# Sums of weight blocks: two of four made by a plain and an accumulating transfer instead of on VectorE, with the lower row of blocks counted as negated

## The chip, the cores and the metric

One core of one Trainium2 chip runs one program. The metric is device time in microseconds of one execution, as the median of several runs. All arithmetic is in 32-bit floats; the matmuls take their operands as a high and a low part (type fp32r), so that each product of two matrices is three passes: high by high, low by high and high by low.

## The reference

Two groups of requests (512 and 256 tokens, 768 in all, width 1024) run through a trunk of two layers. Each layer has a feed-forward block (SwiGLU) ahead of and behind a mixer. The change touches only the four feed-forward blocks.

```python
def swiglu(h, wg, wu, wd):                  # wg, wu: 1024 x 2816; wd: 2816 x 1024
    return (jax.nn.silu(h @ wg) * (h @ wu)) @ wd

def even_layer(x, ...):                     # the odd layer is alike, with another mixer
    x = x + 0.5 * swiglu(rmsnorm(x, f1_n), f1_g, f1_u, f1_d)
    x = x + mixer_ab(rmsnorm(x, mix_n), ...)
    x = x + 0.5 * swiglu(rmsnorm(x, f2_n), f2_g, f2_u, f2_d)
    return x
```

## The kernel before

**Layout.** The activations lie transposed: 8 tiles of 128 features by 768 tokens (`x0` to `x7`), cut into two halves of 384 tokens. The feed-forward width of 2816 is worked in 11 pairs of 2 x 128 columns (function `pair`); behind every second pair a stage `down` multiplies what two pairs (the first time one) left by their rows of the down matrix. The last two pairs go through `down_last`, in the ordinary way.

**Seven products instead of eight.** Within a pair, a weight matrix is a 2 x 2 arrangement of blocks `a11`, `a12` (upper row: the first 128 output columns, by the two halves of the 1024 inputs) and `a21`, `a22` (lower row: the second 128 output columns). A block is 128 x 512 floats, 256 KB. With the activations cut in 2 x 2 as well, Winograd's form of Strassen's method needs seven block products, named p1 to p7 in the code, each with one weight operand and one activation operand (`b11`, `b21`, `t1`, `t2`, `t3`, `b22`, `n4`). Three of the weight operands are blocks (`a11`, `a12`, `a22`), four are sums of blocks, which VectorE makes in the function `sums` (line 579 of the profile):

```python
s1 = a21 + a22;   s2 = s1 - a11;   s3 = a11 - a21;   s4 = a12 - s2
```

A pair needs them for the gate and the up matrix, a `down` stage for its pairs, so a full stage makes eight sums. Each operand then is split in a high part (`whi`, ScalarE, L115) and a low part (`wlo`, VectorE, L116) ahead of its 12 matmuls per matrix.

**Buffers.** The weight blocks arrive from memory in tiles `raw` of 512 KB (four buffers; two blocks of one row of the arrangement per tile). The sums lie in tiles `s` (eight buffers, handed out in turn). The split parts lie in `whi` and `wlo` (five buffers each). All transfers are issued by SyncE (queue SP), in one order; a transfer into a buffer waits until the readers of what was in it are done, and what stands behind it in the queue waits with it.

**The beginning of a block.** The first three pairs are early: their products p1 and p2 run on the first token half while the norm is still being worked out, in the order of the table `ORDER`; then each goes through p6, p7, p5, p3, p4. The later pairs go p1, p6, p2, p7, p5, p3, p4 (the very last in an order of its own). The norm's scale comes from a matmul with ones (`ps_aux<-ones,acc`), a small VectorE step and a power on GpSimd (`sm<-sm,minus`, L254), and three transposes on TensorE (`ps_aux<-ident,sm`, L152).

**Order of the work.** TensorE's order is written out by the program (a planner with generators and delays). The other engines' orders come from a scheduler that knows which values each instruction needs and estimates when they are there.

Of the kernel before, what the change touches and what calls it, by code (L numbers as in the profile page):

```python
# [48 lines left out]
class Trunk:  # L49
# [54 lines left out]

    def wsplit(self, src, eng=None, keep=False):
# [8 lines left out]
        hi, lo = (t.rearrange("p (a b) -> p a b", a=src.shape[1]) for t in (hi, lo))  # L114
        nc.scalar.copy(hi, src)  # L115
        (eng or nc.gpsimd).tensor_tensor(out=lo, in0=src, in1=hi.bitcast(F32), op=ALU.subtract)  # L116
        return hi, lo
# [179 lines left out]
    def feed(self, m, h):  # L297


        nc = self.nc  # L300
        c0, c1 = HALVES[h]
        k = m % 4
        x = self.x[m][:, c0:c1]
        if h == 0:
            self.gain_split("b11" if m < 4 else "b21", k, x, m)
            return
        if "work" not in self.guards:
            self.unfed.append(m)
            return
        t = self.tmp[m] = self.etile("tmp")  # L310
        if m < 4:
            nc.vector.tensor_tensor(out=t, in0=x, in1=self.x[m][:, :H], op=ALU.subtract)
        else:
            nc.scalar.activation(t, x, AF.Copy, scale=self.gain(m))
        if k in self.tmp and k + 4 in self.tmp:
            t2 = self.tmp["t2", k] = self.etile("tmp")
            self.combine(t2, self.tmp[k], -1, k, self.tmp[k + 4])
            self.split(*self.b["t2"][k], t2)
            if len(self.tmp) == KD + 4:
                self.made += ["t2"]  # L320

    def gain_split(self, n, k, src, m):

        hi, lo = self.b[n][k]
        self.nc.scalar.activation(hi, src, AF.Copy, scale=self.gain(m))
        self.nc.vector.scalar_tensor_tensor(
            out=lo, in0=src, scalar=self.gain(m), in1=hi.bitcast(F32), op0=ALU.mult, op1=ALU.subtract
        )

    def combine(self, out, x, sign, m, other):  # L330

        g, op = (self.gain(m), ALU.subtract) if sign > 0 else (self.gain(m, self.ngains), ALU.add)
        self.nc.vector.scalar_tensor_tensor(out=out, in0=x, scalar=g, in1=other, op0=ALU.mult, op1=op)  # L333
# [10 lines left out]
    def rest(self, after):  # L344
# [5 lines left out]
        for n in ("t3", "t1", "b22", "n4"):  # L350
            for k in range(4):
                with self.tc.issue_after(self.copied[after - 1]) if after else nullcontext():
# [6 lines left out]
                    elif n == "n4":  # L359
                        t = self.tmp["t2", k]  # L360
                        self.combine(t, self.x[k + 4][:, a0:a1], 1, k + 4, t)
# [27 lines left out]
    def ffn(self, pre):  # L389
# [8 lines left out]
        d, dl = {}, {}  # L398

        def operands(q):  # L400


            h = hs.pop(q)
            sub = lambda o, x, y: nc.vector.tensor_tensor(out=o, in0=x, in1=y, op=ALU.subtract)
            d[q] = {}
# [6 lines left out]
            yield put("b11", h11)  # L412
            yield sub(h11, h12, h11)
            yield put("t1", h11)
            yield put("b21", h21)
            yield sub(h11, h22, h11)
            if q and q % 2 == 0:
                self.later = operands_2(h, sub, put)
                return
            for _ in operands_2(h, sub, put):  # L420
                yield

        def operands_2(h, sub, put):
            h11, h12, h21, h22 = h[0, 0], h[0, 1], h[1, 0], h[1, 1]
# [3 lines left out]
            yield put("b22", h22)  # L428
            yield sub(h21, h21, h11)
            yield put("n4", h21)  # L430

        def pair(p):
# [5 lines left out]
            def load(tiles):  # L438
                for n in names:
                    for i in tiles:  # L440
                        r = self.first.pop(0) if self.first else self.raw(f"{pre}_w_{n}", 0, KD, (2 * p + i) * P, P)
                        a[n, i + 1, 1], a[n, i + 1, 2] = r[:, 0:4, :], r[:, 4:8, :]

# [4 lines left out]
            def sums(n, name):  # L448
                return self.sums(a[n, 1, 1], a[n, 1, 2], a[n, 2, 1], a[n, 2, 2], s, n, name)

# [23 lines left out]
            def hidden(i, half, g, u):  # L474
# [5 lines left out]
                nc.vector.tensor_tensor(out=t, in0=g, in1=r, op=ALU.mult)  # L480
                nc.scalar.activation(t, t, AF.Silu)
                nc.vector.tensor_tensor(out=v, in0=u, in1=r, op=ALU.mult)
                nc.vector.scalar_tensor_tensor(out=t, in0=t, scalar=0.5, in1=v, op0=ALU.mult, op1=ALU.mult)  # L483

# [51 lines left out]
            if early:  # L536
# [6 lines left out]
                yield  # L543
            load((0, 1))
            if p:
# [30 lines left out]

    def sums(self, a11, a12, a21, a22, s, n, name):

        f = lambda o, x, y, op: self.nc.vector.tensor_tensor(out=o, in0=x, in1=y, op=op)  # L579
        if name == "s1":  # L580
            return s[n, "s1"]
        if name == "s4":
            t = s[n, "s2"]
            f(t, a12, t, ALU.subtract)
            return t
# [3 lines left out]
        t = s[n, name] = self.fw.tile([P, 4, P], F32, tag="s", name=name, bufs=8)  # L589
        if name == "s3":  # L590
            f(t, a11, a21, ALU.subtract)
        else:
            f(t, s[n, "s1"], a11, ALU.subtract)
        return t

    def dtile(self, name):
        return self.fw.tile([P, H], F32R, tag="e", name=f"d{name}", bufs=NE)

    def down(self, pre, pairs, d, acc):
# [3 lines left out]
        nc = self.nc  # L603
        a, s, bank = {}, {}, {}
        for p in pairs:
            rows = [self.raw(f"{pre}_w_down", 2 * p + k, 1, 0, D)[:, 0, :] for k in (0, 1)]
            a[p] = [t[:, i * 512 : (i + 1) * 512].rearrange("p (a b) -> p a b", a=4) for i in (0, 1) for t in rows]
        sums = lambda name: {p: self.sums(*a[p], s, p, name) for p in pairs}
# [27 lines left out]

        w = {n: {p: a[p][i] for p in pairs} for i, n in enumerate(("a11", "a12", "a21", "a22"))}
        s2 = sums("s2")
# [11 lines left out]
    def last_operands(self, d, k0, h, acc=None):  # L650

        todo = [(j, o) for o in ((0, 1), (1, 1)) for j in range(4)] if acc else []
        for half in (0, 1):
            for i in (0, 1):
# [3 lines left out]
                for j, (f, g) in todo[:3]:  # L658
                    x = self.x[4 * f + j][:, HALVES[g][0] : HALVES[g][1]]
                    self.nc.vector.tensor_tensor(out=x, in0=x, in1=acc[j], op=ALU.add)  # L660
                    yield
# [936 lines left out]
```

## Time and profile before

| | |
|---|---|
| median of 3 runs | 2640.08 us (2638.77 to 2641.93) |
| the profiled execution | 2645.25 us, its span 2643.5 us |
| granted TensorE clock, mean | 0.993 |
| TensorE busy | 2586.7 us, 98% |
| VectorE busy | 2225.4 us, 84% |
| ScalarE busy | 1357.5 us, 51% |
| GpSimd busy | 97.6 us, 4% |
| moved by transfers | 214.27 MB, mean 81 GB/s |

Busy is the time between the start and the end of an engine's instructions. Matmuls overlap, so the count of matmuls in a stretch of time tells more than the busy share. The row of a wait tells which engine sat idle, and which instruction ended the wait. The last three columns in a table of stretches are the granted clock, the mean busy share of the 16 transfer engines, and the rate. The powers of the norms at 531.68, 777.03, 1276.64, 1788.49, 2120.11 and 2616.15 us mark the stages: the feed-forward blocks lie from 0 to 531, 777 to 1277, 1277 to 1788 and 2120 to 2616 us, the mixers between.

### The profile page before, as it was taken

How to read it: one execution, taken by the hardware profiler on the slowest of the kernel's cores; microseconds unless marked ns; L12 is line 12 of the kernel's file. 1: busy time of each engine (PE TensorE's matmuls, PEld its weight loads, DVE VectorE, ACT ScalarE, POOL GpSimd, SP SyncE). 2: the span in 40 equal slices, each digit the busy share in tenths (PEclk: the TensorE clock that was granted, in tenths of full speed). 3: DMA queues.
4: the chain of work that ended last, by engine and by line, in shares of the span. 5: the costliest groups of instructions: out<-in, count | busy, mean ns of one | idle time of the engine just before them, and what ended most of it. 6: DMA issues, size and time to landing. Idle time of an engine off the chain costs nothing.

```text
span 2643.5 us, 40905 instructions
## 1 busy us (share of the span) xinstructions
PE 2586.7 (98%) x15180; PEld 2515.4 (95%) x15180; DVE 2225.4 (84%) x4447; ACT 1357.5 (51%) x2808; POOL 97.6 (4%) x139
## 2 busy tenths in 40 slices
PE   8999999999999999999999999999999999999998
PEld 7899999987898999999999999998998989999998
DVE  8988889878869988889898888985667589888886
ACT  6545444546746544545654544464555455454443
POOL 0000000000000000000000000002212100000000
PEclk9999999999999999999999999999999999999999
DMA  5433222321132222223232222232112222222221
GB/s 156 125 81 93 80 73 71 126 89 51 47 101 91 80 65 79 67 78 96 64 96 64 76 69 75 69 129 80 60 62 72 80 80 80 80 65 80 64 81 63
DMA packets 83176, 214.27 MB, mean 81 GB/s; under 512 B 20128, under 2 KB 32928, under 8 KB 82976
## 3 DMA queue, kind: packets, MB, share of 16 engines
q1 hardware_dynamic: 82832, 211.62, 25.8%
q8 instruction: 119, 1.95, 0.3%
q14 instruction: 81, 0.66, 0.1%
q10 hardware_dynamic: 144, 0.03, 0.0%
HBM read 202.18 MB, written 15.07 MB: 82 GB/s over the span
## 4 chain that ended last, share of the span: by engine, by line
PE 68%; DVE 4%; ACT 2%; issue 1%; DMA 1%; POOL 0%; DVEq 0%; ACTq 0%; SPq 0%; POOLq 0%
PE ps_mm L141 42%; PE ps_aux L141 25%; PE ps_aux L152 1%; DMA raw<-in_w 1%; DVE wlo L116 1%; DVE s L579 1%; DVE ol L205 0%; ACT whi L115 0%; DVE tmp L333 0%; DVE x L631 0%; ACT ug L1157 0%; ACT L1157 0%; ACT p L884 0%; ACT L884 0%; DVE sg L483 0%
## 5 line engine op out<-in xcount | busy, mean ns | idle before, releaser
L115 ACT CAST whi<-s 128x512 fp32r<-128x512 f32 x496 | 301.7, 620 | 392.8 <-DVE s L579 142.8
L115 ACT CAST whi<-raw 128x512 fp32r<-128x512 f32 x512 | 312.5, 619 | 284.9 <-PE ps_mm L141 134.1
L116 DVE TENSOR_TENSOR wlo<-s,whi 128x512 fp32r<-128x512 f32 x496 | 336.0, 686 | 77.3 <-ACT whi L115 75.2
L116 DVE TENSOR_TENSOR wlo<-raw,whi 128x512 fp32r<-128x512 f32 x494 | 335.8, 686 | 38.6 <-ACT whi L115 35.9
L141 PE MATMUL ps_mm<-db,whi 128*128 128x384 f32 x864 | 221.3, 337 | 0.0
L141 PE MATMUL ps_aux<-dt,whi 128*128 128x384 f32 x864 | 221.3, 337 | 0.0
L141 PEld LDWEIGHTS ps_aux<-dt,whi 128*128 128x128 f32 x864 | 156.8, 188 | 0.0
L141 PEld LDWEIGHTS ps_mm<-db,whi 128*128 128x128 f32 x864 | 156.8, 188 | 0.0
L141 PE MATMUL ps_aux<-dt,wlo 128*128 128x384 f32 x432 | 145.7, 337 | 0.4 <-DVE wlo L116 0.4
L141 PE MATMUL ps_mm<-db,wlo 128*128 128x384 f32 x432 | 145.6, 337 | 0.0
L141 PE MATMUL ps_mm<-xh,whi 128*128 128x512 f32 (+1 forms) x416 | 145.3, 349 | 0.0
L141 PE MATMUL ps_mm<-xl,whi 128*128 128x512 f32 (+1 forms) x416 | 141.0, 339 | 0.0
L141 PE MATMUL ps_mm<-xh,wlo 128*128 128x512 f32 (+1 forms) x416 | 140.9, 339 | 0.0
L466 ACT COPY u<-ps_mm 128x384 f32<-128x384 f32 x176 | 83.5, 475 | 41.6 <-PE ps_mm L141 41.4
L471 DVE TENSOR_TENSOR u<-ps_aux,u 128x384 f32<-128x384 f32 x176 | 97.3, 553 | 6.9 <-PE ps_aux L141 4.5
L579 DVE TENSOR_TENSOR s<-raw 128x512 f32<-128x512 f32 x124 | 85.1, 686 | 17.3 <-DMA raw<-in_w 17.2
L579 DVE TENSOR_TENSOR s<-raw,raw 128x512 f32<-128x512 f32 x124 | 83.3, 686 | 19.4 <-DMA raw<-in_w 19.4
L141 PE MATMUL ps_aux<-dh,whi 128*128 128x384 f32 x384 | 98.9, 339 | 0.0
L631 DVE TENSOR_TENSOR x<-ps_aux,x 128x384 f32<-128x384 f32 x160 | 86.9, 554 | 12.3 <-PE ps_aux L141 12.2
L884 ACT ACTIVATE p<-p,st 128x256 f32<-128x256 f32 (+3 forms) x144 | 69.1, 481 | 47.8 <-DVE st L879 47.7
L631 DVE TENSOR_TENSOR x<-ps_mm,x 128x384 f32<-128x384 f32 x160 | 87.1, 552 | 6.0 <-PE ps_mm L141 6.0
L141 PEld LDWEIGHTS ps_mm<-xh,whi 128*128 128x128 f32 x416 | 78.9, 190 | 9.8 <-issue 1.0
(477 smaller groups left out, 8030.8 us busy)
## 6 DMA issues: line engine op xcount, KB each, us to landing
raw<-in_w SPq DMA_DIRECT2D x338, 512.0 KB, 3.7
xdm<-x SPq DMA_DIRECT2D x16, 384.0 KB, 2.4
raw<-in_w SPq DMA_DIRECT2D x16, 256.0 KB, 4.0
x<-in_x SPq DMA_DIRECT2D x16, 192.0 KB, 4.6
xold<-xdm SPq DMA_DIRECT2D x8, 384.0 KB, 3.0
x<-xdm SPq DMA_DIRECT2D x8, 384.0 KB, 3.5
out_y<-y SPq DMA_DIRECT2D x8, 384.0 KB, 2.6
tab<-skew SPq DMA_DIRECT2D x8, 256.0 KB, 4.2
```

Source lines behind the costliest of these rows:

```text
L115: nc.scalar.copy(hi, src)
L116: (eng or nc.gpsimd).tensor_tensor(out=lo, in0=src, in1=hi.bitcast(F32), op=ALU.subtract)
L141: self.nc.tensor.matmul(out, lhsT=lhsT, rhs=rhs, start=start, stop=stop, **kw)
L152: self.nc.tensor.transpose(out, src, self.ident)
L466: nc.scalar.copy(e[n, out], bank[key, n])
L471: nc.vector.tensor_tensor(out=t, in0=bank[key, n], in1=t, op=ALU.add)
L579: f = lambda o, x, y, op: self.nc.vector.tensor_tensor(out=o, in0=x, in1=y, op=op)
L631: nc.vector.tensor_tensor(out=o, in0=ps, in1=o, op=ALU.add)
L884: nc.scalar.activation(outs[i - n0], outs[i - n0], AF.Exp, scale=-1.0, bias=mn[:, i : i + 1], accum_out=sm[:, i : i + 1])
```

## The change

Two of the four sums are made by transfers. For `s1` and `s3`, SyncE issues a plain transfer of one block into the tile `s`, and GpSimd then issues a second transfer that adds the other block to what is there. So that both are plain additions, the lower row of blocks counts as negated: the sums become `s1 = a21 + a22`, `s3 = a11 + a21`, `s2 = s1 + a11`, `s4 = a12 + s2`. The signs that this brings are taken up where the products and the activations are combined: other subtractions, factors of -1, a scale of -1 inside the activation function, and `x -= product` instead of `+=` for the lower row of outputs. A path of `wsplit` for a negated split comes with it, which nothing calls.

A `raw` tile now holds only blocks that are used as such: (`a11`, `a12`) of gate, of up, and (`a22` of gate, `a22` of up), each tile filled by two transfers of 256 KB. Per matrix and stage seven transfers of one block replace two transfers of two blocks.

```diff
+    def region(self, name, k0, nk, c0, n):
+        ...                                  # the source's place in the weights, and no tile
+    def parts(self, *srcs):
+        raw = self.rawp.tile([P, 512 * len(srcs)], F32, tag="raw", name=f"rawp{len(self.units)}")
+        for i, src in enumerate(srcs):
+            self.nc.sync.dma_start(raw[:, i * 512 : (i + 1) * 512], src)
+        return [raw[:, i * 512 : (i + 1) * 512].rearrange("p (a b) -> p a b", a=4) for i in range(len(srcs))]
+
+    def wsum(self, name, x, y):
+        t = self.fw.tile([P, 4, P], F32, tag="s", name=name, bufs=8)
+        f = t.rearrange("p a b -> p (a b)")
+        self.nc.sync.dma_start(f, x)
+        self.nc.gpsimd.dma_start(f, y, accum_op=ALU.add)
+        return t
...
             yield put("b11", h11)
-            yield sub(h11, h12, h11)
+            yield sub(h11, h11, h12)
             yield put("t1", h11)
             yield put("b21", h21)
-            yield sub(h11, h22, h11)
+            yield less(h11, h11, h22)
...
+            def load_all():
+                r = {
+                    (n, i): self.region(f"{pre}_w_{n}", 0, KD, (2 * p + i) * P, P)
+                    for n in names for i in (0, 1)
+                }
+                q = {(n, i + 1, k + 1): r[n, i][:, k * 512 : (k + 1) * 512] for n, i in r for k in (0, 1)}
+                for n in names:
+                    a[n, 1, 1], a[n, 1, 2] = self.parts(q[n, 1, 1], q[n, 1, 2])
+                for n in names:
+                    s[n, "s1"] = self.wsum("s1", q[n, 2, 1], q[n, 2, 2])
+                for n in names:
+                    s[n, "s3"] = self.wsum("s3", q[n, 1, 1], q[n, 2, 1])
+                a["gate", 2, 2], a["up", 2, 2] = self.parts(q["gate", 2, 2], q["up", 2, 2])
...
-                nc.scalar.activation(t, t, AF.Silu)
+                nc.scalar.activation(t, t, AF.Silu, scale=-1.0 if i else 1.0)
...
-            load((0, 1))
+            load_all()
...
+    def sums(self, a11, a12, s, n, name):
+        f = lambda o, x, y: self.nc.vector.tensor_tensor(out=o, in0=x, in1=y, op=ALU.add)
         if name == "s2":
-            t = s[n, "s1"] = self.fw.tile([P, 4, P], F32, tag="s", name="s1", bufs=8)
-            f(t, a21, a22, ALU.add)
...
+            t = s[n, "s2"] = self.fw.tile([P, 4, P], F32, tag="s", name=name, bufs=8)
+            f(t, s[n, "s1"], a11)
+        elif name == "s4":
+            f(s[n, "s2"], a12, s[n, "s2"])
...
+                    elif out is not acc and out[0]:
+                        nc.vector.tensor_tensor(out=o, in0=o, in1=ps, op=ALU.subtract)
...
```

TensorE's instructions and their order are the same in both programs, apart from the names of buffers. The places where the other engines' orders differ, and of which the prediction speaks, are two.

**ScalarE, in the first feed-forward block, at the p6 of the second pair.** Here `u<-ps_mm` copies a finished product (the gate's p6) out of its accumulator, `sg` is the activation function, `s_859` before and `s_873` after are the up matrix's `s2`. Before:

```order
L481 ACTIVATE sg<-sg 128x384
L115 CAST whi_833<-s_831 128x512
L466 COPY u_849<-ps_mm_827 128x384
L204 CAST db_851<-sg 128x384
L115 CAST whi_861<-s_859 128x512
L115 CAST whi_882<-s_880 128x512
L115 CAST whi_906<-s_904 128x512
```

And after, where `s_836` and `s_839` are the gate's and the up matrix's `s3`, which come by transfers:

```order
L146 CAST whi_849<-s_847 128x512
L146 CAST whi_875<-s_873 128x512
L146 CAST whi_894<-s_836 128x512
L532 ACTIVATE sg<-sg 128x384
L146 CAST whi_916<-s_839 128x512
L146 CAST whi_939<-s_830 128x512
L146 CAST whi_958<-s_833 128x512
L517 COPY u_865<-ps_mm_845 128x384
```

The split of the up matrix's `s2` stood behind the copy of the gate's product, and now stands two instructions ahead of the activation function and six ahead of that copy; splits of transferred sums stand between.

**GpSimd, at the beginning of the first feed-forward block.** Before, its queue there holds the powers for the two token halves, one behind the other (the `x2`):

```order
L1443 TENSOR_SCALAR ngains<-gains 128x56
L254 TENSOR_TENSOR sm<-sm,minus 128x3 x2
L254 TENSOR_TENSOR sm<-sm,minus 128x6
```

After, `s_563` to `s_572` are the sums of the first pair (`s1` of gate and up, `s3` of gate and up), and `s_830` to `s_839` those of the second:

```order
L285 TENSOR_TENSOR sm<-sm,minus 128x3
L127 DMA s_563<-in_w 128x512
L127 DMA s_566<-in_w 128x512
L127 DMA s_569<-in_w 128x512
L127 DMA s_572<-in_w 128x512
L127 DMA s_830<-in_w 128x512
L127 DMA s_833<-in_w 128x512
L127 DMA s_836<-in_w 128x512
L127 DMA s_839<-in_w 128x512
L285 TENSOR_TENSOR sm<-sm,minus 128x3
```

Eight accumulating transfers moved in between the two powers, and the last two of them fill buffers that the first pair's `s1` used.

More of the change, by code (lines that the diff above doesn't have):

```diff
@@ L114, in wsplit @@
         hi, lo = (t.rearrange("p (a b) -> p a b", a=src.shape[1]) for t in (hi, lo))
+        if sign < 0:
+            nc.scalar.activation(hi, src, AF.Copy, scale=-1.0)
+            nc.vector.scalar_tensor_tensor(
+                out=lo, in0=src, scalar=-1.0, in1=hi.bitcast(F32), op0=ALU.mult, op1=ALU.subtract
+            )
+            return hi, lo
         nc.scalar.copy(hi, src)
@@ L448, in sums @@
             def sums(n, name):
[L449 removed]
+                return self.sums(a[n, 1, 1], a[n, 1, 2], s, n, name)
             def product(n, w, b, key, start):
@@ L596, in dtile, with down_parts @@
     def dtile(self, name):
         return self.fw.tile([P, H], F32R, tag="e", name=f"d{name}", bufs=NE)
+    def down_parts(self, pre, pairs, s):
+        q = {p: [self.region(f"{pre}_w_down", 2 * p + k, 1, 0, D) for k in (0, 1)] for p in pairs}
+        part = lambda p, i, k: q[p][k][:, i * 512 : (i + 1) * 512]
+        w = {n: {} for n in ("a11", "a12", "a22")}
+        for p, t in zip(pairs, self.parts(*[part(p, 0, 0) for p in pairs])):
+            w["a11"][p] = t
+        for p in pairs:
+            s[p, "s1"] = self.wsum("s1", part(p, 1, 0), part(p, 1, 1))
+        for p in pairs:
+            w["a12"][p], w["a22"][p] = self.parts(part(p, 0, 1), part(p, 1, 1))
+        for p in pairs:
+            s[p, "s3"] = self.wsum("s3", part(p, 0, 0), part(p, 1, 0))
+        return w
@@ L599, in down @@
     def down(self, pre, pairs, d, acc):
         nc = self.nc
[L604 to L608, printed above, removed]
+        s, bank = {}, {}
+        w = self.down_parts(pre, pairs, s)
+        sums = lambda name: {p: self.sums(w["a11"][p], w["a12"][p], s, p, name) for p in pairs}
@@ L659, in last_operands @@
                     x = self.x[4 * f + j][:, HALVES[g][0] : HALVES[g][1]]
-                    self.nc.vector.tensor_tensor(out=x, in0=x, in1=acc[j], op=ALU.add)
+                    self.nc.vector.tensor_tensor(out=x, in0=x, in1=acc[j], op=ALU.subtract if f else ALU.add)
                     yield
```

56 lines of the change are left out of this document (27 added, 29 removed).

## The prediction

> **What bounds the kernel now.** I read the busy times first, then the chain that ended last, to see which engine sets the end.
>
> ```profile
> PE 2586.7 (98%) x15180; PEld 2515.4 (95%) x15180; DVE 2225.4 (84%) x4447; ACT 1357.5 (51%) x2808; POOL 97.6 (4%) x139
> PE 68%; DVE 4%; ACT 2%; issue 1%; DMA 1%; POOL 0%; DVEq 0%; ACTq 0%; SPq 0%; POOLq 0%
> ```
>
> TensorE (PE) carries the chain; VectorE (DVE) appears in it with 4%. The change takes no matmul away, so what it can win is TensorE's lost time in the feed-forward blocks. For that I read TensorE's stretches, one steady (the second row) and the four in which it waits; in brackets stands the count of matmuls, behind it the granted clock.
>
> ```profile
> 40.00:125.00 85.00, 73.71 (x394) 0.96 0.33 98
> 300.00:400.00 100.00, 100.00 (x569) 1.00 0.24 74
> 800.00:880.00 80.00, 71.97 (x390) 0.98 0.23 73
> 1365.00:1375.00 10.00, 8.96 (x50) 1.00 0.14 53
> 2148.00:2226.00 78.00, 70.11 (x374) 0.96 0.24 75
> ```
>
> The steady row has 100 us / 569 = 0.1757 us per matmul and no idle time: nothing to win there. At that pace the other rows' counts are worth 69.2, 68.5, 8.8 and 65.7 us; the rest of their widths is lost: 15.8 + 11.5 + 1.2 + 12.3 = 40.8 us. That is the whole stock. Of it 11.29 + 8.03 + 1.04 + 7.89 = 28.3 us is idle time (width less busy); the rest are slower matmuls behind the waits, where the clock column shows 0.96 and 0.98. So a microsecond of idle time costs 40.8 / 28.3 = 1.44 us.
>
> Who was waited for, over the whole execution:
>
> ```profile
> PE ps_mm L141 <- ACT whi L115: 15.6, 13, 3.0
> PE ps_mm L141 <- DVE wlo L116: 10.0, 12, 1.8
> PE ps_aux L141 <- DVE wlo L116: 3.0, 3, 1.4
> ```
>
> 28.6 us in 28 waits, and all for the split parts of weights. The larger single ones, from the timeline of TensorE (in brackets the wait, and for whom):
>
> ```profile
> 44.04 0.44 PE L141 MATMUL ps_mm<-t20h,whi 128*128 128x384 f32 x1 [3.05 <-ACT whi L115]
> 63.81 0.45 PE L141 MATMUL ps_aux<-b220h,wlo 128*128 128x384 f32 x1 [1.42 <-DVE wlo L116]
> 68.02 0.44 PE L141 MATMUL ps_mm<-n40h,wlo 128*128 128x384 f32 x1 [1.84 <-DVE wlo L116]
> 79.14 0.44 PE L141 MATMUL ps_mm<-t20h,whi 128*128 128x384 f32 x1 [1.50 <-ACT whi L115]
> 117.03 0.45 PE L141 MATMUL ps_mm<-t20h,whi 128*128 128x384 f32 x1 [1.50 <-ACT whi L115]
> 828.84 0.44 PE L141 MATMUL ps_mm<-n40h,wlo 128*128 128x384 f32 x1 [1.11 <-DVE wlo L116]
> 837.79 0.44 PE L141 MATMUL ps_mm<-t20h,whi 128*128 128x384 f32 x1 [1.50 <-ACT whi L115]
> 877.77 0.45 PE L141 MATMUL ps_mm<-t20h,whi 128*128 128x384 f32 x1 [1.50 <-ACT whi L115]
> 2155.95 0.44 PE L141 MATMUL ps_mm<-t30h,whi 128*128 128x384 f32 x1 [1.09 <-ACT whi L115]
> 2170.63 0.45 PE L141 MATMUL ps_aux<-b220h,wlo 128*128 128x384 f32 x1 [1.15 <-DVE wlo L116]
> 2174.84 0.44 PE L141 MATMUL ps_mm<-n40h,wlo 128*128 128x384 f32 x1 [1.84 <-DVE wlo L116]
> 2182.59 0.44 PE L141 MATMUL ps_mm<-t20h,whi 128*128 128x384 f32 x1 [1.50 <-ACT whi L115]
> 2222.16 0.45 PE L141 MATMUL ps_mm<-t20h,whi 128*128 128x384 f32 x1 [1.50 <-ACT whi L115]
> ```
>
> The moving operand's name tells the product: `t20h` is p6 with the weight `s2`, `t30h` p7 with `s3`, `b220h` p3 with `s4`, `n40h` p4 with `a22`. Six waits are 1.50 us to the hundredth: the same order each time. VectorE and ScalarE show it at the second and the third pair's p6:
>
> ```profile
> 71.38 0.56 DVE L480 TENSOR_TENSOR sg<-ps_mm,acc 128x384 f32<-128x384 f32 x1 [2.34 <-PE ps_mm L141]
> 76.92 0.69 DVE L579 TENSOR_TENSOR s<-s,raw 128x512 f32<-128x512 f32 x1
> 115.57 0.48 ACT L466 COPY u<-ps_mm 128x384 f32<-128x384 f32 x1 [4.16 <-PE ps_mm L141]
> 116.36 1.14 ACT L115 CAST whi<-s 128x512 fp32r<-128x512 f32 x2
> ```
>
> VectorE idles 2.34 us for a product, and makes the up matrix's `s2` only at 76.92. At 115.57 ScalarE waits until TensorE has finished the gate's product, copies it, does one more thing, and only at 116.36 splits the weight that TensorE wants next. A split queued behind a copy of the product just ahead of it cannot but stall TensorE.
>
> **The change part by part.** *Two sums less on VectorE.* The rows that go, and two of the combinations whose forms are exchanged for each other:
>
> ```profile
> L579 DVE TENSOR_TENSOR s<-raw 128x512 f32<-128x512 f32 x124 | 85.1, 686 | 17.3 <-DMA raw<-in_w 17.2
> L579 DVE TENSOR_TENSOR s<-raw,raw 128x512 f32<-128x512 f32 x124 | 83.3, 686 | 19.4 <-DMA raw<-in_w 19.4
> L483 DVE SCALAR_TENSOR_TENSOR sg<-sg,v 128x384 f32<-128x384 f32 x88 | 48.6, 552 | 0.9 <-ACT sg L481 0.5
> L404 DVE TENSOR_TENSOR u<-u,u 128x384 f32<-128x384 f32 x36 | 20.0, 556 | 0.8
> 1400.00:1500.00 100.00, 100.00 (x568) 100.00 (x567) 86.77 (x158) 48.08 (x96) 0.00 (x0) 1.00 0.25 74
> ```
>
> 248 sums of 686 ns, 168 us, leave VectorE, and with them the two kinds that waited for transfers (17.2 + 19.4 us). In the steady stretch (last row: TensorE 100.00, VectorE 86.77 of 100 us) that wins nothing, since TensorE never waits there. The changed signs cost nothing: 552 against 556 ns, and a scale inside an activation that ran anyway.
>
> *The order at the block beginnings.* ScalarE's new order shows, at the second pair, the up matrix's split ahead of the copy; VectorE's new order has both `s2` ahead of the `sg` for which it idled at 71.38. I followed every split in both orders and counted how many matmuls TensorE has queued between the product that ScalarE or VectorE must await first and the split's first use. Of the thirteen waits quoted, eight no longer stand behind such a copy or addition: 79.14, 117.03, 837.79, 877.77, 2182.59, 2222.16 (1.50 each), 2155.95 (1.09) and 2170.63 (1.15), together 11.24 us. Four still do: 63.81, 68.02, 828.84, 2174.84, together 6.21 us; these I leave as they are, late because VectorE is full of the activation function's steps. Of the stock of 28.3 us 10.8 us remain, small waits and the 3.05 us at 44.04. There the wanted `s2` needs one sum instead of two, and the pair's other sums no longer stand between. The bounds are none and all; I take half, 5.4 us, since VectorE loses four of a pair's eight sums. Idle time gone: 11.24 + 5.4 = 16.6 us; at 1.44, 24 us. If the 5.4 were 0 or 10.8: 16 or 32 us.
>
> *The transfers.* Per full stage SyncE issues ten transfers of 256 KB instead of four of 512 KB, and GpSimd four that accumulate. What a landing takes:
>
> ```profile
> raw<-in_w SPq DMA_DIRECT2D x338, 512.0 KB, 3.7
> raw<-in_w SPq DMA_DIRECT2D x16, 256.0 KB, 4.0
> q1 hardware_dynamic: 82832, 211.62, 25.8%
> ```
>
> So a plain one takes about 4 us. No row shows an accumulating one. If it cost no more than a plain one, 4 us; if it cost as two one after the other (it must read the tile and the block), 8 us; nearer is 4 us, since in these rows bytes hardly count. The Trainium skill, "Collectives: The Full Stack", section "The bandwidth ceiling: the fold count and why AG ≠ RS ≠ AR", says that an add in a transfer costs two source reads, and not the add itself; by it 512 KB would be read for a block, which by the first row is 3.7 us and leaves the sum as it is; no run here shows it yet. The load: 248 tiles of 512 KB (130 MB) become 372 + 248 plain blocks (163 MB) and 248 accumulated ones (65 MB, 130 if counted twice): (211.6 + 33 + 130) / 211.6 x 25.8% = 46% of the 16 engines. The cover is the buffers. A stage is 168 matmuls, 29.5 us; the next stage's `s1` goes into buffers that the stage before left, some 20 us ahead, its `s3` into those of this stage's `s1`, split about half a stage ahead. Against 8 to 12 us for a plain and an accumulating transfer in a row this holds; without it, the first rival comes. Behind a waiting `s3` in SyncE's queue stand the next `raw` tiles; these wait for parts of the same stage anyway, and there are three per stage instead of four for four buffers.
>
> *GpSimd's queue.* In it the norm's power for the second token half now stands behind transfers, in the first and third block behind the second pair's `s3`, which need the first pair's `s1` split.
>
> ```profile
> 53.73 0.68 DVE L116 TENSOR_TENSOR wlo<-s,whi 128x512 fp32r<-128x512 f32 x1
> 56.59 1.23 POOL L254 TENSOR_TENSOR sm<-sm,minus 128x3 f32<-128x3 f32 x1 [32.06 <-DVE sm L253]
> 59.43 0.38 PE L152 MATMUL ps_aux<-ident,sm 128*128 128x128 f32 x2
> 1315.79 1.23 POOL L254 TENSOR_TENSOR sm<-sm,minus 128x3 f32<-128x3 f32 x1 [38.05 <-DVE sm L253]
> 1320.58 0.49 PE L152 MATMUL ps_aux<-ident,sm 128*128 128x128 f32 x3
> ```
>
> The last split of the first pair's `s1` ended at 54.4; a plain transfer of 4 us puts the accumulating one at 58.4, the power's end (1.23) at 59.6 or, with the issue, 60 to 61, against the transposes at 59.43. TensorE's order is fixed, so it would wait 1 to 2 us there; in the third block the slack, 1320.58 - 1317.02 = 3.6 us, covers it. Bounds: 0, and 5 us (8 us instead of 4 for the transfer). I take 1.5 us, at 1.44 some 2 us.
>
> Sum: -24 + 2 = -22 us. The profiled execution, 2645.25 us with a span of 2643.5, would become 2623; it lies 5.2 us above the median of the runs, 2640.08, which becomes 2618.
>
> **The rivals.** *1. The accumulating transfers cannot keep up (slower).* Four per stage of 29.5 us: one at a time, 7.4 us each is where it decides. At 9 us a stage takes 36, 6.5 us more, and with 62 full stages (11 pairs and 4.5 `down` per block) that is 400 us, some 3040 us; at 8 us, 2.5 x 62 = 155 us, 2795. For it speaks that no accumulating row exists; against it the 4 us above, and that plain ones overlap. The mechanism could also be a GpSimd that gets to write its orders only while VectorE pauses, 13 us in 100 by the row of the steady stretch, or 3.9 us for four a stage. The Trainium skill, "SBUF — State Buffer", section "SBUF: two separate sides", has that rule: transfers issued by GpSimd starve while VectorE runs in a mode that takes both ports. By its list (section "Who interferes with whom") an addition of two tensors has no such mode, and such additions are what VectorE runs here; the two rows of 552 and 686 ns for 384 and 512 elements, 1.05 ns per further element, show no faster mode. Chance 0.15.
>
> *2. Only the transfers' delay moves (same).* The sums come late enough at the beginnings that ScalarE, in whose order splits of transferred sums stand ahead of the copies, waits for them instead: the 24 us are won and lost again, at 12 late sums of about 1.4 us of idle time. Time 2636 to 2645. Against it: the second pair's `s1` goes into buffers that nothing has used, a whole pair ahead of its use. Chance 0.09.
>
> *3. Everything goes.* VectorE's relief also ends the four waits that I leave: 28.3 us of idle time, the whole 40.8 us: 2599. Against it: these waits stand behind additions (`u<-ps_aux,u`), not sums. Chance 0.06.
>
> *4. The forecast,* 10 to 33 us faster, 2607 to 2630: chance 0.70.
>
> **How the numbers follow.** The time is the forecast's, 2618. Below 2602 lies most of rival 3 (0.05), above 2645 lie rival 1 (0.15) and little else; the range is 2602 to 2645. A measurement of this kernel tells a change of about 0.2%, 5 us, from none. Faster: 0.70 + 0.06, less some of the forecast's low end, 0.75; same: 0.08; slower: 0.15 from rival 1 and the other side of rival 2, 0.17.
>
> **What would show it.** Right: the waits of 1.50 us before `t20h` are gone, those before `n40h` stay; TensorE's steady stretch still has 569 matmuls in 100 us; VectorE is busy about 2060 us; GpSimd's transfers land within 4 to 8 us. Wrong: splits that wait for an `s` from a transfer, TensorE idle in the steady stretch, or more than 3 us of waiting at the transposes of `sm`.

## The result, and the profile after

The changed kernel takes 2620.78 us (median of 4 runs, 2619.57 to 2625.45) against 2639.6 beside it: a ratio of 0.9929, 95% interval 0.9917 to 0.9941. A second series on another occasion gave 2621.06 and 0.9925 (0.9913 to 0.9938). The profiled execution, the slowest of the four, took 2625.45 us, its span 2623.7, 19.8 less than before.

The lines of the page that answer to those before: busy times, the chain that ended last, the two transfer queues (packets, MB, share of 16 engines), the issues with the median time from issue to landing, and GpSimd's time to issue an accumulating one (917 ns).

```profile
PE 2580.4 (98%) x15180; PEld 2516.2 (96%) x15180; DVE 2096.2 (80%) x4199; ACT 1367.7 (52%) x2808; POOL 315.0 (12%) x387
PE 71%; DVE 2%; ACT 1%; issue 1%; DMA 1%; POOL 0%; SPq 0%; DVEq 0%; ACTq 0%; POOLq 0%
q1 hardware_dynamic: 136400, 244.15, 29.5%
q0 software_dynamic: 35712, 65.03, 16.0%
rawp<-in_w SPq DMA_DIRECT2D x372, 256.0 KB, 3.9
s<-in_w SPq DMA_DIRECT2D x248, 256.0 KB, 3.1
s<-in_w POOLq DMA_DIRECT2D x248, 256.0 KB, 4.9
L127 POOL DMA_DIRECT2D s<-in_w x248 | 217.3, 917 | 1464.2 <-DVE wlo L147 325.1
```

VectorE's share of the chain fell from 4% to 2%. The transfers are 45.5% of the engines' time instead of 25.8%. TensorE's stretches, one steady (the second row) and the beginnings of the first three blocks:

```profile
40.00:125.00 85.00, 79.81 (x434) 0.96 0.74 179
300.00:400.00 100.00, 100.00 (x569) 1.00 0.54 131
790.00:870.00 80.00, 77.88 (x446) 1.00 0.61 156
1350.00:1360.00 10.00, 10.00 (x59) 1.00 0.64 174
```

The steady stretch holds the same 569 matmuls, with the transfer engines busy 0.54 instead of 0.24. The first block's beginning has 434 matmuls in 85 us instead of 394; the third's has no idle time left. TensorE's waits in the beginnings, from its timeline; in brackets the wait, and for whom:

```profile
42.20 0.44 PE L172 MATMUL ps_mm<-t20h,whi 128*128 128x384 f32 x1 [2.16 <-ACT whi L146]
66.08 0.44 PE L172 MATMUL ps_mm<-n40h,wlo 128*128 128x384 f32 x1 [1.83 <-DVE wlo L147]
781.14 0.69 PE L172 MATMUL ps_mm<-b110h,whi 128*128 128x384 f32 x1 [3.54 <-ACT whi L146]
823.61 0.44 PE L172 MATMUL ps_mm<-n40h,wlo 128*128 128x384 f32 x1 [1.11 <-DVE wlo L147]
2132.05 0.55 PE L172 MATMUL ps_aux<-b210h,whi 128*128 128x384 f32 x1 [4.99 <-ACT p L547]
2158.79 0.44 PE L172 MATMUL ps_mm<-n40h,wlo 128*128 128x384 f32 x1 [1.90 <-DVE wlo L147]
```

All six waits of 1.50 us are gone; those before `n40h` stand within 0.06 us. Two are new in size, at the openings of the two blocks behind mixers (781 and 2132 us; before 0.62 and 1.48 us). Counted along TensorE's fixed order, after less before, the time comes and goes so: first block -8.0 us; opening of the second +5.1; the rest of it -9.3; third block -1.3; a slow drift of some -3 in its steady part; opening of the fourth +4.7; the rest of it -8.5. So -27 inside the blocks and +9.8 at the two openings (each number to some 0.3 us, by where an opening is taken to end). Two of these vary from execution to execution: in the second series the openings cost some 0.6 and 5.8 us, and e1 below, whose waits are those of before, drifts by -2.3 us in the same steady part, so that the drift isn't the change's.

For the experiments one number per profile is enough: the waits of TensorE added up over the four beginnings (26 to 130, 770 to 890, 1285 to 1400 and 2100 to 2240 us). It is 29.99 before and 18.22 after (16.65 in the second series).

### The profile page after: what moved, and what is told of

Its sections match the earlier page's. It is cut to its first block, busy times and chain, and to the rows that moved or that the text cites. A ratio compares the mean times of both kernels' runs of the same rounds, so it can differ in the third digit from the quotient of the medians.

```text
span 2623.7 us, 41959 instructions
## 1 busy us (share of the span) xinstructions
PE 2580.4 (98%) x15180; PEld 2516.2 (96%) x15180; DVE 2096.2 (80%) x4199; ACT 1367.7 (52%) x2808; POOL 315.0 (12%) x387
## 3 DMA queue, kind: packets, MB, share of 16 engines
q1 hardware_dynamic: 136400, 244.15, 29.5%
q0 software_dynamic: 35712, 65.03, 16.0%
## 4 chain that ended last, share of the span: by engine, by line
PE 71%; DVE 2%; ACT 1%; issue 1%; DMA 1%; POOL 0%; SPq 0%; DVEq 0%; ACTq 0%; POOLq 0%
PE ps_mm L172 44%; PE ps_aux L172 26%; PE ps_aux L183 1%; DVE wlo L147 0%; DVE ol L236 0%; DMA s<-in_w 0%; DMA raw<-in_w 0%; ACT ug L1213 0%; ACT whi L146 0%; ACT L1213 0%; ACT p L940 0%; DVE tmp L366 0%; ACT L940 0%; ACT oh L235 0%; DVE y L289 0%
## 5 line engine op out<-in xcount | busy, mean ns | idle before, releaser
L127 POOL DMA_DIRECT2D s<-in_w x248 | 217.3, 917 | 1464.2 <-DVE wlo L147 325.1
L146 ACT CAST whi<-rawp 128x512 fp32r<-128x512 f32 x324 | 199.0, 620 | 251.5 <-issue 106.5
L147 DVE TENSOR_TENSOR wlo<-rawp,whi 128x512 fp32r<-128x512 f32 x324 | 222.6, 687 | 22.4 <-ACT whi L146 15.2
L146 ACT CAST whi<-raw 128x512 fp32r<-128x512 f32 x188 | 115.6, 619 | 110.3 <-PE ps_mm L172 74.8
L147 DVE TENSOR_TENSOR wlo<-raw,whi 128x512 fp32r<-128x512 f32 x170 | 115.9, 687 | 28.0 <-ACT whi L146 26.7
L686 DVE TENSOR_TENSOR x<-x,ps_aux 128x384 f32<-128x384 f32 x160 | 86.4, 550 | 12.0 <-PE ps_aux L172 12.0
L630 DVE TENSOR_TENSOR s<-s,rawp 128x512 f32<-128x512 f32 x124 | 84.9, 687 | 10.7 <-DMA rawp<-in_w 7.9
```

What stands on the lines that cost most here:

```text
L127: self.nc.gpsimd.dma_start(f, y, accum_op=ALU.add)
L630: f = lambda o, x, y: self.nc.vector.tensor_tensor(out=o, in0=x, in1=y, op=ALU.add)
L686: nc.vector.tensor_tensor(out=o, in0=o, in1=ps, op=ALU.subtract)
```

## The experiments

Each was timed beside the kernel before. "Idle" is the sum just named.

| | us, median | ratio (95%) | idle | VectorE busy |
|---|---|---|---|---|
| before | 2640 | 1 | 29.99 | 2225.4 |
| after, second series | 2621.06 | 0.9925 (0.9913 to 0.9938) | 16.65 | 2094.9 |
| e1 signs alone | 2641.01 | 0.9999 (0.9990 to 1.0008) | 29.68 | 2225.0 |
| e2 rows first | 2642.91 | 1.0010 (1.0001 to 1.0019) | 31.31 | 2217.1 |
| e3 sums behind raw | 2629.86 | 0.9956 (0.9944 to 0.9969) | 21.16 | 2097.0 |
| e4 no s1, no s3 | 2624.38 | 0.9935 (0.9923 to 0.9948) | 17.96 | 2091.3 |
| f2 first pair old | 2622.90 | 0.9927 (0.9914 to 0.9939) | 16.83 | 2100.8 |
| f3 s1 only by transfer | 2637.24 | 0.9984 (0.9975 to 0.9993) | 24.05 | 2155.0 |
| f4 s3 only by transfer | 2648.38 | 1.0025 (1.0016 to 1.0034) | 30.05 | 2157.2 |
| g1 no s1 | 2630.47 | 0.9961 (0.9949 to 0.9974) | 22.06 | 2153.9 |
| g2 no s3 | 2639.18 | 0.9998 (0.9989 to 1.0007) | 27.36 | 2160.8 |
| g3 accumulated twice | 2674.28 | 1.0127 (1.0112 to 1.0143) | 50.22 | 2095.4 |
| g4 n4 first | 2618.25 | 0.9918 (0.9904 to 0.9932) | 16.58 | 2095.2 |

A straight line through these and the first profile of after is 2594.8 us + 1.60 x idle; no kernel lies further from it than 5.5 us, and all but f3 and f4 within 3.3. The sum leaves out two larger waits that lie behind its windows, 4.25 us in g3 (at 138.72 us) and 2.12 us in f4 (at 260.64 us). With the waits behind the windows counted too (the final norm's left out), the line is 2598.1 us + 1.44 x idle, and none lies further from it than 4.6 us. So TensorE's waits are nearly the whole effect, at 1.44 to 1.60 us for each microsecond.

**e1: the signs alone.** The changed kernel's signs, with all sums on VectorE and the loads of before.

```diff
-                for n in names:
-                    s[n, "s1"] = self.wsum("s1", q[n, 2, 1], q[n, 2, 2])
...
+            f(s[n, "s1"], a21, a22)          # on VectorE; s3 alike
```

> Only the signs: the lower row counts as negated, all four sums stay on VectorE, and the weights are loaded as before (512 KB tiles, the gate's two rows, then the up matrix's two). Theory A (the gain comes from sums leaving VectorE and arriving by transfer) expects no change: 2640 us, within 5 us, with the six waits of 1.50 us before t20h still there. If the signs themselves did anything, the time would move towards 2621.

Measured 2641.01 us, 0.9999. Within 0.1%, the signs cost and bring nothing.

**e2: the order of loading alone.** The change also moved the transfers: before, the gate's upper and lower rows came ahead of the up matrix's; now both upper rows come first. That alone, in the kernel before:

```diff
-                for n in names:
-                    for i in tiles:
+                for i in tiles:
+                    for n in names:
```

In the order this does to ScalarE what the prediction quoted: the up matrix's split of `s2` stands ahead of the copy of the gate's product. ScalarE in e2, first block, second pair:

```
L115 CAST whi_833<-s_831 128x512
L115 CAST whi_861<-s_859 128x512
L115 CAST whi_882<-s_880 128x512
L115 CAST whi_906<-s_904 128x512
L466 COPY u_849<-ps_mm_827 128x384
L204 CAST db_851<-sg 128x384
```

> The kernel before, with two loops exchanged: the upper rows of the gate and of the up matrix are loaded ahead of both lower rows, instead of the gate's two rows ahead of the up matrix's. All sums stay on VectorE, nothing is added in a transfer. Theory A (VectorE's relief and the transferred sums took the waits away) expects 2640 us, within 5, and the waits before t20h still there. Rival B (the waits came from the order of loading, which the change also altered) expects the eight waits of the prediction, 11.24 us of idle time, to go: at 1.44 us each some 16 us, 2624 us, with VectorE still busy about 2225 us.

Measured 2642.91 us: theory A's time, without the gain of rival B, though the order is the one that B wanted. But the waits didn't stay as theory A had them. TensorE at the second pair, then VectorE, from the timelines of e2:

```profile
76.41 0.44 PE L141 MATMUL ps_mm<-t20h,whi 128*128 128x384 f32 x1 [3.02 <-ACT whi L115]
...
73.42 0.56 DVE L482 TENSOR_TENSOR v<-ps_mm,acc 128x384 f32<-128x384 f32 x1 [1.93 <-PE ps_mm L141]
73.90 0.68 DVE L579 TENSOR_TENSOR s<-raw 128x512 f32<-128x512 f32 x1
74.50 0.55 DVE L483 SCALAR_TENSOR_TENSOR sg<-sg,v 128x384 f32<-128x384 f32 x1
74.97 0.69 DVE L579 TENSOR_TENSOR s<-s,raw 128x512 f32<-128x512 f32 x1
75.57 0.69 DVE L579 TENSOR_TENSOR s<-raw 128x512 f32<-128x512 f32 x1
76.29 0.69 DVE L579 TENSOR_TENSOR s<-s,raw 128x512 f32<-128x512 f32 x1
```

The gate's `s2` (ended 75.7) now waits behind the addition `v`, which waits 1.93 us for a product, and needs two sums. The six waits of 1.50 us are gone, and others of up to 3.02 us stand at the gate's `s2`, a product earlier. In the changed kernel the same place reads:

```profile
67.01 1.29 DVE L630 TENSOR_TENSOR s<-s,rawp 128x512 f32<-128x512 f32 x2
68.80 0.56 DVE L531 TENSOR_TENSOR sg<-ps_mm,acc 128x384 f32<-128x384 f32 x1 [0.50 <-PE ps_mm L172]
```

Both `s2` are done at 68.3, one sum each, ahead of the step that waits for the product. For this place the changed kernel has both the order and the shorter work.

**e3: the opening, by the queue.** At 781 us ScalarE, in after, waits for a weight of an early pair. Its transfer stands in SyncE's queue behind four plain ones of the first pair's sums, which wait for TensorE's work in the mixer; theory C takes that place in the queue for the cause. SyncE's queue in after (start, time, and how many):

```profile
767.02 4.25 SPq L126 DMA_DIRECT2D s<-in_w  x4
773.57 10.02 SPq L96 DMA_DIRECT2D raw<-in_w  x3
```

So those four were queued behind the tiles.

```diff
+                with nullcontext() if p else self.tc.issue_after(self.last_raw):
+                    for n in names: s[n, "s1"] = self.wsum("s1", q[n, 2, 1], q[n, 2, 2])
...
```

> The changed kernel, with the plain transfers of a block's first pair's sums queued behind the last weight tile of the early pairs on SyncE. Theory C (at the openings of the two blocks behind mixers SyncE waits for the sums' buffers while the early pairs' weights stand behind) expects the waits of 3.54 us at 781 and of 4.99 us at 2132 to go, and most of the 9.8 us lost at these openings: 2611 to 2615 us. Rival D (the openings lose because the transfers compete or land late) expects 2620 us, within 3.

Measured 2629.86 us, 9 us worse than after. Both theories missed the time, and theory C falls: of the wait at 781 us 0.38 us is left, but that at 2132 us stayed, with 4.29 us, and a longer one than both came 18 us behind the first.

The traces show that the place in the queue didn't make this weight late. Behind the four, SyncE waited in after for the mixer's VectorE to free the tile's own buffer; before the change it issued the same tile at the same point, at 781.54 us, where everything stood 7.97 us later. What differs is the landing. SyncE's wait in after, from 771.5 to 774 us, and the tile's transfer in before and in after:

```profile
SPq L96 <- DVE x L880: 2.3, 1, 2.3
...
raw<-in_w SPq DMA_DIRECT2D x1, 512.0 KB, 4.0
...
raw<-in_w SPq DMA_DIRECT2D x1, 512.0 KB, 6.9
```

It landed 2.9 us later, and TensorE waited 2.9 us longer (3.54 instead of 0.62). In the second series it took 4.7 us, with a wait of 1.34; in e3, with the sums' transfers moved away from beside it, 3.7. So the transfers compete, as rival D has it.

TensorE and VectorE at the new wait, two stretches (the last two columns are the share of the transfer engines and GB/s), and the accumulating transfers from 770 to 800 us, all in e3:

```profile
799.17 0.69 PE L172 MATMUL ps_aux<-b210h,whi 128*128 128x384 f32 x1 [5.42 <-ACT p L547]
...
796.92 0.69 DVE L630 TENSOR_TENSOR s<-s,rawp 128x512 f32<-128x512 f32 x1 [7.15 <-DMA s<-in_w]
...
780.00:785.00 5.00, 5.00 (x30) 1.00 0.94 350
785.00:790.00 5.00, 5.00 (x31) 1.00 1.07 382
...
s<-in_w POOLq DMA_DIRECT2D x6, 256.0 KB, 9.1
```

VectorE's fixed order has the sum `s2` in it, and stands still for 7.15 us until the transferred `s1` is there; ScalarE's copy `p` stands behind, and TensorE behind that. And the transfer engines are full in these 10 us. From issue to landing the six accumulating transfers of this opening took 9.1 us (the median), against 4.9 over the whole execution of after. The wait at 2132 us in after has the same two parts: the engines were busy 0.90 and 1.10 from 2110 to 2120 us, and VectorE's order held an `s2` whose block, a plain transfer, landed late:

```profile
2121.39 0.69 DVE L630 TENSOR_TENSOR s<-s,rawp 128x512 f32<-128x512 f32 x1 [7.91 <-DMA rawp<-in_w]
```

**e4, g1, g2: VectorE's relief without a transfer.** The kernel before, with both sums left out, or one.

```diff
         if name == "s1":
-            return s[n, "s1"]
+            return a21
...
         if name == "s3":
-            f(t, a11, a21, ALU.subtract)
+            return a11
```

> The kernel before, with the sums s1 and s3 left out: the products that need them take a21 and a11 instead, s2 becomes a21 - a11. No transfer is added, and the loads stand as before, so only VectorE's relief of 168 us is left of the change. Theory A expects most of the gain inside the blocks, 20 us or more, and no loss at the openings: 2612 to 2622 us. Rival B (order of loading) expects the waits before t20h to stay, and a gain of at most the 5.4 us of small waits: 2632 to 2640 us.

> The kernel before with the sum s1 alone left out (a21 is taken in its place) and no transfer added: VectorE loses 85 us. Beside f3, where the same sum comes by transfers and 2637 us were measured. Theory G (the transfers of s1 cost what VectorE's relief brings) expects 2625 to 2632 us. Theory H (half of the relief brings little, because it leaves the s2 of the second pair behind the activation's steps in VectorE's order) expects 2634 to 2640 us.

> The kernel before with the sum s3 alone left out (a11 is taken in its place) and no transfer added. Beside f4, where the same sum comes by transfers and 2648 us were measured. Theory G expects 2632 to 2638 us, so that the transfers of f4 cost some 12 us. Theory H expects 2640 us or more, as in f4.

Both out: 2624.38 us, so the relief alone brings 16 of the 19 us. Alone, `s1` brings 9.6 us (2630.47, theory G), `s3` 0.9 (2639.18, between the theories): `s2` needs `s1`, and `s3` only stands in its way; that the two together bring more than 9.6 + 0.9 us these runs don't explain. Counted along TensorE's order, e4 gains some 20.5 us inside the blocks, where after gains 27, and loses some 1.5 us at the two openings, where after loses 9.8. Inside, e4 keeps the old order of loading: at the second pair the up matrix's `s2` is still made behind the gate's product, in the timeline of e4:

```profile
76.41 0.69 PE L141 MATMUL ps_mm<-t20h,whi 128*128 128x384 f32 x1 [4.07 <-ACT whi L115]
```

That this order makes the difference inside is argued; no run joins it to e4.

**f3, f4: one sum by transfer.** The rows are loaded whole as before, and one sum comes by a plain and an accumulating transfer beside them, so that a matrix costs six blocks of transfer in place of the seven of the change and the four of before.

```diff
+                for n in names:
+                    if "s1" in BYDMA:
+                        s[n, "s1"] = self.wsum("s1", q[n, 2, 1], q[n, 2, 2])
```

> Only s1 by a plain and an accumulating transfer; s3 is made on VectorE from whole rows, loaded as before. Theory A (a second s2 must come out of one sum instead of two, and soon) expects most of the gain inside the blocks, since s2 needs s1: 2618 to 2628 us, with VectorE at 2160 us. If both sums were worth the same, half of the gain: 2631 us.

> Only s3 by a plain and an accumulating transfer; s1 stays on VectorE. Theory A expects little: s2 still needs two sums on VectorE, and in the orders five splits for t20h still stand behind the copy of the gate's product, so 2632 to 2638 us. If both sums were worth the same, half of the gain: 2631 us.

2637.24 and 2648.38 us, each above what was expected of it. Beside g1 and g2 the transfers cost 6.8 and 9.2 us, which the whole change doesn't show (it is 3.3 us faster than e4). One place where they cost is the second block's opening, in f3:

```profile
789.62 0.44 PE L175 MATMUL ps_mm<-b110h,whi 128*128 128x384 f32 x1 [2.44 <-ACT whi L149]
```

In g1 a wait of 0.30 us stands there. The others, by the timelines: in f3 TensorE waits 4.07 us at 77.68 us and 1.90 us at 116.14, where g1 has 2.88 and nothing. In f4 it waits 4.79 us at 81.12 us and 3.10 at 2149.14 (g2: 3.95 and 1.12), and 2.12 us at 260.64 us, in a stretch where no other kernel waits more than 0.38 us; that one the idle sum leaves out. All are waits for splits or copies; how much of them late transfers caused, and how much the changed orders, these runs don't settle. f3 and f4 are also the two that lie 4.0 and 5.5 us above the first line.

**f2: the opening, by the bytes.** The changed kernel, with the first pair of the two blocks behind mixers loaded and summed in the old way.

```diff
+                if p == 0 and pre.endswith("ffn2"):
+                    for n, i in r:
+                        a[n, i + 1, 1], a[n, i + 1, 2] = self.whole(r[n, i])
+                    return
```

> The changed kernel once more, as the measure for the three beside it: 2621 us, within 3.

> The changed kernel, with the first pair of the two blocks behind mixers loaded and summed in the old way (four tiles of 512 KB, all four sums on VectorE). Theory E (at these openings the transfer engines are the bound: 14 blocks for the first pair instead of 8, with the early pairs' weights beside them) expects the waits of 3.54 us at 781 and 4.99 us at 2132 to go, one or two short waits of the old kind to come back (1 to 2 us each), and 2612 to 2616 us. Rival F (the openings lose because of the changed order on VectorE and ScalarE, not because of bytes) expects 2618 to 2624 us.

2622.90 against 2621.06 us beside it, no difference: theory F's number, but not for its reason. The two waits shrink to 0.50 and 1.73 us, near those of before, and old ones come back:

```profile
798.92 0.44 PE L172 MATMUL ps_mm<-t20h,wlo 128*128 128x384 f32 x1 [2.84 <-DVE wlo L147]
...
2128.10 0.44 PE L172 MATMUL ps_aux<-b210h,whi 128*128 128x384 f32 x1 [1.73 <-ACT p L551]
2139.08 0.44 PE L172 MATMUL ps_mm<-t30h,whi 128*128 128x384 f32 x1 [1.09 <-ACT whi L146]
2153.57 0.45 PE L172 MATMUL ps_aux<-b220h,wlo 128*128 128x384 f32 x1 [1.15 <-DVE wlo L147]
```

Counted along TensorE's order, f2 loses nothing at the two openings, and gains 5.6 and 5.9 us in the rest of these blocks, where after gains 9.3 and 8.5. So the opening's loss was a price of that pair's gain, and undoing both wins nothing. How much it is varies: in the second series of after the wait at the second block was 1.34 us instead of 3.54, that at the fourth 4.93.

**g3: how far the cover goes.** Every accumulating transfer twice.

```diff
+        for _ in (0, 1):
             self.nc.gpsimd.dma_start(f, y, accum_op=ALU.add)
```

> The changed kernel, with every accumulating transfer issued twice in a row into the same tile (a block is added twice, so the sums are others). Eight instead of four a stage, each 0.92 us of GpSimd and 4.9 us from issue to landing, the transfer engines busy some 61% instead of 45.5%. The prediction's cover (an accumulated sum is wanted 20 us after its buffer comes free) expects the steady stretch to stay at 569 matmuls in 100 us, and a loss at the four beginnings alone: 2625 to 2640 us. The prediction's first rival (the transfers fall behind from 7.4 us a stage's sum on) expects TensorE to wait in every stage: 2750 us or more.

2674.28 us, 53 more than after: far from the rival, above the range that I gave. The queue of the accumulating transfers, two steady stretches, and three waits of TensorE, with what VectorE waited for at the second:

```profile
q0 software_dynamic: 71424, 130.06, 30.8%
...
300.00:400.00 100.00, 100.00 (x569) 1.00 0.75 168
900.00:1000.00 100.00, 100.00 (x574) 1.00 0.78 172
...
64.47 0.90 PE L184 MATMUL ps_aux<-ident,sm 128*128 128x128 f32 x3 [4.87 <-POOL sm L286]
96.56 0.66 PE L173 MATMUL ps_aux<-b220h,whi 128*128 128x384 f32 x1 [5.13 <-DVE u L523]
1370.46 0.69 PE L173 MATMUL ps_aux<-b220h,whi 128*128 128x384 f32 x1 [7.53 <-DVE u L523]
...
93.25 0.69 DVE L631 TENSOR_TENSOR s<-s,rawp 128x512 f32<-128x512 f32 x1 [6.22 <-DMA s<-in_w]
```

In the two steady stretches nothing is lost with the engines busy 0.75 and 0.78. The beginnings lose 32 to 34 us more of idle time than after, and 4.25 us more follow at 138.72 us: VectorE's order has an `s2` in it that waits 6.22 us for a transferred sum while `u`, for which TensorE waits, stands behind, and at 64.47 the norm's power stands behind accumulating transfers in GpSimd's queue, the wait that the prediction had priced for the single ones.

**g4: the waits that stayed.**

```diff
-                with self.tc.high_priority() if early and b in ("b11", "b21") else nullcontext():
+                with self.tc.high_priority() if early and b in ("b11", "b21", "n4", "b22") else nullcontext():
```

> The changed kernel, with the splits for p4 and p3 (n4 and b22) of the early pairs given precedence in the scheduler, nothing else. The prediction left the waits of 1.83, 1.11 and 1.90 us before n40h as caused by a VectorE full of the activation's steps. If it is the place in VectorE's order and not its load, they go: 4.8 us of idle time, at 1.44 some 7 us, 2614 us against 2621. If VectorE is simply full, the wait moves to the steps behind: 2621 us, within 3.

2618.25 us; its interval overlaps that of after, so a gain isn't shown. The wait moves to the steps behind:

```profile
66.06 0.44 PE L172 MATMUL ps_mm<-n43h,whi 128*128 128x384 f32 x1 [0.93 <-ACT n43h L235]
67.05 0.44 PE L172 MATMUL ps_mm<-n43l,whi 128*128 128x384 f32 x1 [0.55 <-DVE n43l L236]
817.18 0.44 PE L172 MATMUL ps_mm<-n43h,whi 128*128 128x384 f32 x1 [1.77 <-ACT n43h L235]
818.18 0.45 PE L172 MATMUL ps_mm<-n43l,whi 128*128 128x384 f32 x1 [0.56 <-DVE n43l L236]
2151.80 0.44 PE L172 MATMUL ps_mm<-n43h,whi 128*128 128x384 f32 x1 [0.38 <-ACT n43h L235]
2153.26 0.44 PE L172 MATMUL ps_mm<-n43l,whi 128*128 128x384 f32 x1 [1.03 <-DVE n43l L236]
```

These sum to 5.22 us; the three before `n40h` were 1.83 + 1.11 + 1.90 = 4.84.

## Why the prediction was right, and where it was not

- **The stock and the price of idle time.** Right: but for the drift, the time lost and won lies in the beginnings. 1.44 us per idle microsecond was right, or a little low: the lines through the kernels give 1.44 and 1.60, with and without the waits behind the windows.
- **Eight waits go.** They did, all but 0.34 us at one `t30h`, and idle time fell by 11.8 us (13.3 in the second series), where 16.6 was forecast; the openings put 6.4 us back (3.54 - 0.62 + 4.99 - 1.48), so that 18.2 went inside the blocks. But the reason, that splits no longer stand behind a copy, is half of it: e2 has that order without the shorter work, and gained nothing; e4 has the shorter work without the order of loading, and gained 16 us. The fall of VectorE's work, which the prediction called worth nothing in the steady stretch and used only for the 5.4 us of small waits, is the greater part. The shorter work moves the order too, but not all of it: in e4 the gate's `s2` at the second pair starts at 67.03 us, ahead of the `sg` at 68.17, as in the changed kernel, and the up matrix's at 74.96, far behind it.
- **Four waits stay, as VectorE is full.** Right for the three before `n40h`, and g4 bears out the reason. The fourth, 1.42 us at 63.81, became two at the same product, 0.82 us for ScalarE and 0.21 for VectorE.
- **The transfers.** Load: 46% forecast, 45.5% measured. Over the whole execution an accumulating transfer took 4.9 us, 0.9 more than the value taken, far from the 8 of the upper bound and from the 7.4 at which rival 1 decides. The Trainium skill, "Collectives: The Full Stack", section "The bandwidth ceiling: the fold count and why AG ≠ RS ≠ AR", counts two source reads for an add; the engines' share agrees (2.04 times a plain transfer's per byte), the landing is longer than the 3.7 us that this gave. The rule of "SBUF — State Buffer" in the Trainium skill, section "Who interferes with whom", that additions of two tensors leave GpSimd's transfers alone, agrees too: they landed in 4.9 us with VectorE busy 80%.
- **The step that failed: "Against 8 to 12 us for a plain and an accumulating transfer in a row this holds".** The cover was worked out for a running block. At an opening behind a mixer, nothing of an earlier stage covers: the early pairs' weights and the first pair's ten plain and four accumulating transfers come close together, and VectorE's and ScalarE's orders count on them early. There the 4 us taken for a landing failed as well: the weight at 781 us took 6.9, and from 2105 to 2130 us plain transfers of 256 KB took 8.2 us (`rawp`) and accumulating ones 7.9, at the median. That cost +9.8 us, none of which was in the sum; f2, which takes the pair's transfers away, brings the two waits down to 0.50 and 1.73 us.
- **GpSimd's power, +2 us.** It cost nothing. The last accumulating transfers ahead of it, which the sum had at 58.4 us, were issued from 50.28 us on. GpSimd and TensorE in after:

```profile
50.28 1.77 POOL L127 DMA_DIRECT2D s<-in_w  x2 [6.00 <-DMA s<-in_w]
54.77 1.19 POOL L285 TENSOR_TENSOR sm<-sm,minus 128x3 f32<-128x3 f32 x1 [2.72 <-DVE sm L284]
...
57.60 0.49 PE L183 MATMUL ps_aux<-ident,sm 128*128 128x128 f32 x3
```

GpSimd itself waited 2.72 us for VectorE's step, and the transposes waited for nothing. The mechanism exists, as g3's 4.87 us show, but there it had twice the transfers ahead of it.
- **VectorE busy, 2060 us.** It was 2096.2: 129 us less, not 168. Neighbours overlap in the rows (two sums in a row took 1.29 us in the row at 67.01, not 1.37), so a removed one frees less than its duration.
- **The sum.** -24 + 2 became -27 + 9.8, and a drift of -3: misses of opposite sign, so the 2618 was nearer to 2620.78 than its parts deserve, and the drift, which isn't the change's, helped: that nearness is in part luck.

## What to carry to other kernels

When work leaves an engine that is busy 84% and off the bottleneck, don't count its busy time: look where that engine's in-order queue makes the bottleneck wait, and ask whether both the place in the queue and the length of the work ahead of it change. In the changed kernel the transfers that replaced arithmetic cost nothing that shows where a stage of lead stood ahead of them; price them anew at every place where that lead begins at zero, since there many come at once, and each lands late. Split a change into its incidental parts (here the order of loading) before crediting the one in its name.

## What the runs showed of the hardware

- An accumulating transfer of 256 KB cost 0.92 us of GpSimd to issue and 4.9 us from issue to landing, against 3.1 and 3.9 us for plain ones. For the 16 engines it is the dearer: 65.03 MB took 16.0% of them and 244.15 MB of plain ones 29.5%, per byte 2.04 times as much.
- The transfer engines at 0.75 to 0.78 of their time (g3) slowed neither TensorE nor VectorE: 569 and 574 matmuls in 100 us, and 687 ns for a split on VectorE, where it was 686 before. The transfers themselves landed later, plain ones of 256 KB in 4.2 and 4.4 us instead of 3.1 and 3.9, accumulating ones in 5.5 instead of 4.9.
- Transfers that came close together landed late, SyncE's and GpSimd's alike: at the fourth block's opening, with the engines busy 0.90 and 1.10 of their time from 2110 to 2120 us, 8.2 us for plain ones (`rawp`) and 7.9 for accumulating ones.
- The count of matmuls in a steady stretch of 100 us varied from 568 to 576 at a granted clock of 1.00, within one execution and between kernels (568 in before at 1400 us, 576 in e2 at 900 us). That is up to 1.4%, more than the whole change; compare profiles along TensorE's order, and not by their spans alone.
